# A hybrid attention layer: the output projection by Strassen's seven products, with the weights' sums made by accumulating transfers

## The chip, the cores and the metric

The kernel runs on one core of one Trainium2 chip. Its time is the device time in microseconds of one execution. TensorE multiplies, VectorE (DVE) and ScalarE (ACT) work on tiles, GpSimd (POOL) does small vector work and issues one queue of transfers, SyncE (SP) issues the other queue.

## What is computed

The reference is one decoder layer on 512 tokens of width 2048, in float32:

```python
h = rmsnorm(x, norm_pre_g)
qa, ka, va, za, qb, ckv, zb, iq, ik, iw = split(h @ w_in)
o_a = diff_attention(qa, ka, va, ...) * silu(za)      # 8 heads of 128
o_b = dsa_attention(qb, rmsnorm(ckv), iq, ik, iw, ...) * silu(zb)  # 8 heads of 128
y = concat(o_a, o_b) @ w_out                          # 512 x 2048 by 2048 x 2048
return x + rmsnorm(y, norm_post_g)
```

The change concerns the product with `w_out`.

## The kernel before, in words

Every large product is made of float32r matmuls with both operands split into a high and a low part: high times high, high times low, low times high, so three matmuls stand for one. The split is a ScalarE copy to float32r (the high part) and a VectorE subtraction (the low part).

The weights pass through one stream. A list `units` (lines 54 to 81) names every weight block in order of use, 128 x up to 1024 elements each. `load_to` (line 89) issues their loads on SyncE's queue into the tiles `wf` (two buffers), `split_to` (line 103) splits them into `wh` and `wl` (lines 123 and 124, three buffers each), and `use` (line 128) hands out the next unit and moves loads and splits ahead. Inside `lead()` these instructions get a priority up to 600 places earlier, so the scheduler, which orders each engine's instructions at build time by priority and by its own model of time, puts them before their use. The engines then run their orders without changing them.

After the projections come eight heads of group A (lines 547 to 563) and eight of group B (lines 576 to 583). The scheduler lays the projections of the next heads over the softmax of the last ones. In group A each head ends with a norm: a sum of squares through TensorE (lines 508 to 512, the square in the tile `sq`), a power of -0.5 on POOL (`rstd`, line 195), and four transposes on TensorE that spread the result over the partitions (`spread`, line 201), before `go[h]` is scaled (line 516). `go[0..7]` holds group A's output and `go[8..15]` group B's, each 128 features x 512 tokens. The bias strips of the heads come through a DRAM table that POOL's queue writes (`strip`, lines 330 to 336); `sc` holds the selection masks of group B, `pt0a` to `pt3b` the transposed probabilities.

Before the last head, fifteen of the sixteen tiles `go` are split for the projection (`split_o`, line 569, into `hh` and `hl`); the last one after it. The projection (lines 589 to 660) goes over four blocks of 512 columns. For each of eight units of weights (two slices of 128 features) it runs four row tiles of 128 tokens, three matmuls each (lines 600 to 602). `done` (line 604) squares the result on ScalarE with a row sum and multiplies it by the gain. In the last block (lines 619 to 660) the row tiles follow one another, each 48 matmuls (the last one in two halves of 256 columns), and each is finished at once: norm, residual from `xn`, and stores to `out`. The last block's weights are kept in tiles that the heads have left (`last`, line 101).

Of the kernel before, what the change touches and what calls it, by code (L numbers as in the profile page):

```python
# [26 lines left out]
def hybrid_layer(tc, xT, xn, wck, wT, wva, wuv, wo, vecs, gpost, lams, relb, oneh, out):  # L27
    nc = tc.nc
    from contextlib import ExitStack
    with ExitStack() as st:  # L30
# [48 lines left out]
        for n in range(4):  # L79
            for kp in range(8):  # L80
                unit(wo[n, kp], (2, 512))
        stage, ready, flags = {}, {}, {"begin": None}
# [5 lines left out]

        def load_to(n):
            while pos["load"] < min(n, len(units)):  # L90
# [3 lines left out]
                nm, bf = ("wf", 2) if flags["begin"] is not None else ("qk", 4)  # L94
# [6 lines left out]
        last = [("qk", 4)] * 4 + [("v", 3)] * 3 + [("ck0", 1), ("ck1", 1)] + [("wh", 3), ("wl", 3)] * 3 + [("pt0a", 1)]  # L101

        def split_to(n):
            while pos["split"] < min(n, len(units)):
                i = pos["split"]
                load_to(i + 1)
                c = units[i][1][0] * units[i][1][1]
                t = stage.pop(i)
                names = [("wh", 3), ("wl", 3)]
                if i >= len(units) - 8:  # L110
                    names = [last.pop(0), last.pop(0)]
                w = []
                for nm, bf in names:
                    if nm == "pt0a":
                        w.append([S.tile([128, 512], F32R, name=x, bufs=1) for x in ("pt0a", "pt0b")])
                    else:
                        a = S.tile([128, 1024], F32R, name=nm, bufs=bf)
                        w.append([a[:, :512], a[:, 512:]] if units[i][1][1] == 512 else [a[:, :c]])
                m = c // len(w[0])
                with tc.high_priority(lead()):  # L120
                    for q in range(len(w[0])):
                        src = t[:, q * m:(q + 1) * m]
                        nc.scalar.copy(w[0][q], src)  # L123
                        nc.vector.tensor_tensor(w[1][q], src, w[0][q].bitcast(F32), op=OP.subtract)  # L124
                ready[i] = w
                pos["split"] += 1

        def use(ahead=3):
            i = pos["use"]
            pos["use"] += 1  # L130
            if ahead:
                load_to(i + ahead + 1)
                split_to(i + ahead)
            nk, n = units[i][1]
            w = ready.pop(i)
            per = nk // len(w[0])
            return [[w[a][k // per][:, (k % per) * n:(k % per + 1) * n] for k in range(nk)] for a in range(2)]
# [55 lines left out]
        def rstd(dst, ssq, n):  # L193
            nc.vector.tensor_scalar(dst, ssq, 1.0 / n, EPS, op0=OP.mult, op1=OP.add)
            nc.gpsimd.tensor_tensor(dst, dst, mhalf[:, :dst.shape[1]], op=OP.pow)
# [167 lines left out]
        def select():  # L363
            for i in range(1, 4):
                nc.gpsimd.affine_select(sc[i][:, i * 128:], sc[i][:, i * 128:], [[-1, 128]], OP.is_ge, -BIG,
                                        base=0, channel_multiplier=1)
# [136 lines left out]
        def head_a(h, q, k, kl):  # L503
# [3 lines left out]
            sq = tmp("sq", 1)  # L507
# [38 lines left out]

        for h in range(8):
            next(sel, None)
            if h % 2 == 0:
# [17 lines left out]
        oh_, ol_ = [], []  # L567

        def split_o(m):
            a = S.tile([128, 512], F32R, name=f"hh{m}")  # L570
            b = S.tile([128, 512], F32R, name=f"hl{m}")
            split((a, b), go[m])
            oh_.append(a)
            ol_.append(b)
# [12 lines left out]
        ssy = S.tile([128, 4, 4], F32, name="ssy")  # L587
        ys = {}
        for n in range(4):
            gB = S.tile([128, 512], F32, name="strip", bufs=2)  # L590
# [137 lines left out]
```

## Time and profile before

| | before |
|---|---|
| median of three executions | 1054.93 us (1054.83 to 1055.67) |
| the profiled execution, its own time | 1055.42 us |
| its span, first to last instruction | 1053.6 us |
| matmuls | 5425, busy 99% of the span |
| granted TensorE clock, mean | 0.998 |
| VectorE, ScalarE, POOL busy | 54%, 40%, 3% of the span |
| moved by transfers | 116 MB, 110 GB/s on average |

All rows come from the profiled execution. PE is TensorE's matmuls, PEld its weight loads, which run beside them. Matmul records overlap one another, because the next one starts before the last has drained. A row of the timeline gives the start from the span's beginning, the duration, the engine, the line, the operation, its output and inputs, and in brackets the idle time before it with what ended it.

### The profile page before, as it was taken

What the parts mean: (1) busy time and instruction counts of PE and PEld (TensorE: products, weight loads), DVE (VectorE), ACT (ScalarE), POOL (GpSimd) and SP (SyncE); (2) the same over time, 40 slices, a digit from 0 to 9 for tenths busy, and PEclk for the clock granted to TensorE, in tenths of its full rate; (3) what the DMA queues carried; (4) which work ended last, traced back from release to release, by engine and by line L of the source; (5) the groups of instructions that cost most, each with busy time, mean ns of one, the idle gap of its engine ahead of it and who ended that gap; (6) DMA issues with size and microseconds to landing.
All of it is one profiled execution on the core that took longest, in us unless ns stands there. A gap on an engine that the chain in (4) does not pass through costs nothing.

```text
span 1053.6 us, 13903 instructions
## 1 busy us (share of the span) xinstructions
PE 1042.1 (99%) x5425; PEld 897.7 (85%) x5425; DVE 568.0 (54%) x1143; ACT 420.9 (40%) x788; POOL 30.3 (3%) x48
## 2 busy tenths in 40 slices
PE   9999999999999999999999999999999999999997
PEld 6798888988889899899899888888888888888886
DVE  6255554569943474565565466554645484323353
ACT  6543433432223464464464465333323353322320
POOL 0002000000000000000000000000000000000001
PEclk9999999999999999999999999999999999999999
DMA  9535633223222322322222232231223232233445
GB/s 347 203 100 177 227 100 100 86 96 100 91 94 95 100 75 86 98 73 91 82 89 86 75 110 81 84 98 60 92 79 94 77 109 91 91 100 110 137 132 191
DMA packets 37073, 116.09 MB, mean 110 GB/s; under 512 B 4448, under 2 KB 4704, under 8 KB 37008
## 3 DMA queue, kind: packets, MB, share of 16 engines
q1 hardware_dynamic: 35376, 108.88, 32.0%
q0 software_dynamic: 1632, 6.33, 1.9%
q8 instruction: 42, 0.69, 0.3%
q14 instruction: 23, 0.19, 0.1%
HBM read 110.96 MB, written 9.48 MB: 114 GB/s over the span
## 4 chain that ended last, share of the span: by engine, by line
PE 97%; DMA 2%; ACT 0%; DVE 0%; issue 0%; SPq 0%; DVEq 0%; POOL 0%; POOLq 0%; ACTq 0%
PE pj L162 19%; PE pj L161 19%; PE pj L160 19%; PE pj L445 3%; PE pj L444 3%; PE pj L443 3%; PE lg L528 3%; PE av L426 3%; PE pj L600 2%; PE pj L602 2%; PE pj L601 2%; PE tr L415 2%; PE lg L252 2%; PE lg L254 2%; DMA wf<-in_wT_dram 1%; PE lg L602 1%
## 5 line engine op out<-in xcount | busy, mean ns | idle before, releaser
L162 PE MATMUL pj<-hh,wl 128*128 128x512 f32 (+2 forms) x912 | 351.9, 386 | 0.0
L161 PE MATMUL pj<-hl,wh 128*128 128x512 f32 (+2 forms) x912 | 350.8, 385 | 0.0
L160 PE MATMUL pj<-hh,wh 128*128 128x512 f32 (+2 forms) x912 | 350.3, 384 | 0.0
L123 ACT CAST wh<-wf 128x1024 fp32r<-128x1024 f32 (+1 forms) x179 | 162.9, 923 | 389.8 <-PE pj L161 182.5
L124 DVE TENSOR_TENSOR wl<-wf,wh 128x1024 fp32r<-128x1024 f32 (+1 forms) x179 | 189.2, 1068 | 196.6 <-ACT wh L123 196.3
L162 PEld LDWEIGHTS pj<-hh,wl 128*128 128x128 f32 (+1 forms) x912 | 170.7, 187 | 30.8 <-issue 0.9
L161 PEld LDWEIGHTS pj<-hl,wh 128*128 128x128 f32 (+1 forms) x912 | 170.6, 187 | 29.9
L160 PEld LDWEIGHTS pj<-hh,wh 128*128 128x128 f32 (+1 forms) x912 | 170.8, 187 | 29.2
L445 PE MATMUL pj<-wh,hl 128*128 128x256 f32 x256 | 73.0, 285 | 0.0
L443 PE MATMUL pj<-wh,hh 128*128 128x256 f32 x256 | 72.9, 285 | 0.0
L444 PE MATMUL pj<-wl,hh 128*128 128x256 f32 x256 | 72.7, 284 | 0.0
L258 DVE SCALAR_TENSOR_TENSOR tq<-pj,rB 128x512 f32<-128x512 f32 (+1 forms) x40 | 26.6, 664 | 66.1 <-PE pj L162 64.4
L444 PEld LDWEIGHTS pj<-wl,hh 128*128 128x128 f32 x256 | 48.9, 191 | 0.6
L443 PEld LDWEIGHTS pj<-wh,hh 128*128 128x128 f32 x256 | 48.9, 191 | 0.4
L445 PEld LDWEIGHTS pj<-wh,hl 128*128 128x128 f32 x256 | 48.8, 191 | 0.1
L601 PE MATMUL pj<-wl,hh 128*128 128x512 f32 x96 | 37.5, 391 | 0.0
L528 PE MATMUL lg<-ck,qk 128*128 128x256 f32 (+3 forms) x192 | 37.4, 322 | 0.0
L600 PE MATMUL pj<-wh,hh 128*128 128x512 f32 x96 | 37.3, 391 | 0.0
L602 PE MATMUL pj<-wh,hl 128*128 128x512 f32 x96 | 37.2, 390 | 0.0
L528 PEld LDWEIGHTS lg<-ck,qk 128*128 128x128 f32 x192 | 32.0, 189 | 3.5
L538 ACT ACTIVATE a<-a,mx 128x128 f32<-128x128 f32 (+3 forms) x32 | 17.9, 561 | 38.5 <-DVE mx L537 38.5
L397 DVE SCALAR_TENSOR_TENSOR sc<-e,iw,sc 128x256 f32<-128x256 f32 (+2 forms) x45 | 27.7, 615 | 7.4 <-ACT e L393 4.8
(343 smaller groups left out, 1414.9 us busy)
## 6 DMA issues: line engine op xcount, KB each, us to landing
wf<-in_wT_dram SPq DMA_DIRECT2D x111, 512.0 KB, 3.5
wf<-in_wo_dram SPq DMA_DIRECT2D x32, 512.0 KB, 3.5
wf<-in_wva_dram SPq DMA_DIRECT2D x16, 512.0 KB, 3.5
table<-bd POOLq DMA_DIRECT2D x16, 320.0 KB, 11.1
go<-in_xT_dram SPq DMA_DIRECT2D x16, 256.0 KB, 6.1
v<-in_xn_dram SPq DMA_DIRECT2D x8, 512.0 KB, 5.1
strip<-table SPq DMA_DIRECT2D x16, 256.0 KB, 3.4
out_dram<-go SPq DMA_DIRECT2D x16, 256.0 KB, 3.6
```

The costliest lines, as they stand in the source:

```text
L123: nc.scalar.copy(w[0][q], src)
L124: nc.vector.tensor_tensor(w[1][q], src, w[0][q].bitcast(F32), op=OP.subtract)
L160: nc.tensor.matmul(ps, a, x, start=(k == 0), stop=False)
L161: nc.tensor.matmul(ps, a, y, start=False, stop=False)
L162: nc.tensor.matmul(ps, b, x, start=False, stop=(k == KT - 1))
L443: nc.tensor.matmul(o, hh[kk][:, ts], wh[k], start=(kk == 0 and i % 2 == 0), stop=False)
L444: nc.tensor.matmul(o, hh[kk][:, ts], wl[k], start=False, stop=False)
L445: nc.tensor.matmul(o, hl[kk][:, ts], wh[k], start=False, stop=(kk == 15 and i % 2 == 1))
L528: nc.tensor.matmul(bank[:, :w], q[u][:, x, i * 128:(i + 1) * 128], ck[u][:, y, :w], start=(n == 0), stop=(n == 5))
L600: nc.tensor.matmul(banks[i], oh_[kk][:, ts], wh[k], start=(kk == 0), stop=False)
L601: nc.tensor.matmul(banks[i], oh_[kk][:, ts], wl[k], start=False, stop=False)
L602: nc.tensor.matmul(banks[i], ol_[kk][:, ts], wh[k], start=False, stop=(kk == 15))
```

## The change

The 512 x 2048 activations are cut into quarters (256 tokens x 1024 features: A11 and A12 are the first 256 tokens of groups A and B, A21 and A22 the last 256), and for each half of the output columns (a pass `p`) the weights are cut into four blocks of 1024 features x 512 columns. Each pass then takes seven products of quarters in place of eight: `a11`, `a12`, `a22`, `d1` = A22 - A21, `e2` = d1 + A11, `s3` = e2 - A22 and `s4` = e2 - A12, each with one weight block or one sum T1 to T4 of blocks. The seven results are added up to the four output blocks.

- The sums T1 to T4 lie in DRAM tiles `tw`. `combine` makes them by transfers on POOL's queue: four copies and four accumulations for each pass and each of four units, 64 transfers of 512 KB. One step is issued in each head (`sums`), behind POOL's last instruction so far: four copies and two accumulations in the heads 0, 2, 4 and so on, two accumulations in the others.
- The stream has 56 units for the projection instead of 32. `wf` gets three buffers instead of two, and `ck1` as a fourth after the heads. Only two units are loaded before the last head has been written down, since the others may read `tw`.
- The activations' sums are made by VectorE and POOL: `d1` in `go[h]` after each head of group B (on POOL, in the last head on VectorE); `e2`, `s3` and `s4` after the last head, eight slices through two temporaries each, then split into tiles that the heads have left.
- A product is 2 row tiles x 8 slices x 3 matmuls. Its result is copied (ScalarE) or subtracted (VectorE, some on POOL) into tiles. The last product of the second pass runs row tile by row tile, the second one in halves.
- `sq` takes a buffer of the ring `tq`.

```diff
-        for n in range(4):
-            for kp in range(8):
-                unit(wo[n, kp], (2, 512))
+        plain = len(units)
+        B11, B12, B21, B22, T1, T2, T3, T4 = range(8)
+        tw = {(p, f, u): DR.tile([128, 1024], F32, name=f"tw{p}{f}{u}")
+              for p in range(2) for f in (T1, T2, T3, T4) for u in range(4)}
+        ORDER = ((("a11", B11), ("d1", T1), ("e2", T2), ("s3", T3), ("s4", B22), ("a22", T4), ("a12", B21)),
+                 (("a11", B11), ("e2", T2), ("s3", T3), ("a22", T4), ("d1", T1), ("s4", B22), ("a12", B21)))
+        for p in range(2):
+            for _, f in ORDER[p]:
+                for u in range(4):
+                    unit(wo[p, f, u] if f < 4 else tw[p, f, u], (2, 512))
+        ring = [("wf", 3)] * 3
...
+        def combine(p, u):
+            def add(dst, src):
+                nc.gpsimd.dma_start(tw[p, dst, u], wo[p, src, u] if src < 4 else tw[p, src, u], accum_op=OP.add,
+                                    max_dma_last_dim=1024)
+            for dst, src in ((T1, B11), (T3, B12), (T2, B11), (T4, B21)):
+                nc.gpsimd.dma_start(tw[p, dst, u], wo[p, src, u])
+            add(T1, B12)
+            add(T3, B22)
+            yield
+            add(T2, T3)
+            add(T4, T2)
+            yield
...
-            sq = tmp("sq", 1)
+            sq = tmp()
...
+        combos = (None for p in range(2) for u in range(4) for _ in combine(p, u))
+        def sums():
+            with tc.issue_after(flags["pool"].ins):
+                next(combos)
         for h in range(8):
             next(sel, None)
+            sums()
...
         for h in range(8):
             if h % 2 == 0:
                 project_vb(h // 2)
+            sums()
             q = [project_qk(1.0 / 16), project_qk(1.0 / 16)]
             if h == 7:
-                for m in range(15):
-                    split_o(m)
+                for j in range(7):
+                    split_x(j, slice(0, 512))
+                split_x(7, lo)
             head_b(h, q)
-        split_o(15)
+            eng = nc.gpsimd if h < 7 else nc.vector
+            flags["pool"] = eng.tensor_tensor(go[h][:, up], go[8 + h][:, up], go[h][:, up], op=OP.subtract)
+        flags["limit"] = len(units)
+        ring.append(("ck1", 1))
+        split_x(7, up)
...
+        for j in range(8):
+            t = S.tile([128, 512], F32, name=("pt0b", "sc3")[j % 2])
+            s3 = S.tile([128, 256], F32, name=("pt2a", "pt2b")[j % 2])
+            nc.vector.tensor_tensor(t[:, up], go[j][:, up], go[j][:, lo], op=OP.add)
+            nc.gpsimd.tensor_tensor(s3, t[:, up], go[8 + j][:, up], op=OP.subtract)
+            nc.gpsimd.tensor_tensor(t[:, lo], t[:, up], go[8 + j][:, lo], op=OP.subtract)
+            z = S.tile([128, 2, 512], F32R, name=zhome[j][0], bufs=zhome[j][1])
+            split((z[:, 0, :], z[:, 1, :]), t)
+            split((ws[j][:, 0, :], ws[j][:, 1, :]), s3)
...
+        def product(form):
+            ps = [bank(), bank()]
+            for u in range(4):
+                w = use()
+                for i in range(2):
+                    part(ps[i], form, i, u, w)
+            return ps
...
+            P1 = product("a11")
+            for i in range(2):
+                nc.scalar.copy(ra[i], P1[i])
+            if p == 0:
+                P5 = product("d1")
+                for i in range(2):
+                    nc.scalar.copy(rb_[i], P5[i])
+                P6 = product("e2")
+                for i in range(2):
+                    sub(rc_[i], P6[i], ra[i])
+                P7 = product("s3")
+                for i in range(2):
+                    sub(rd[i], rc_[i], P7[i])
+                    sub(rc_[i], rc_[i], rb_[i], nc.gpsimd)
+                    sub(rb_[i], rd[i], rb_[i], nc.gpsimd)
+                    done(rb_[i], 2 + i, n2, gBs[1])
...
+                cuts = (0, 512) if i == 0 else (0, 256, 512)
                 for a, b in zip(cuts, cuts[1:]):
...
+                    ps = bank()[:, cs]
+                    for u in range(4):
+                        part(ps, "a12", i, u, w[u], cs)
+                    nc.vector.tensor_tensor(ra[i][:, cs], ps, ra[i][:, cs], op=OP.add)
+                    square(ra[i][:, cs], i, n1)
+                    more(ry if b == 512 else base, i, n1, base)
+                    nc.vector.tensor_tensor(ra[i][:, cs], ra[i][:, cs], gBs[0][:, cs], op=OP.mult)
+                final(i, ry, xs[i])
```

In the first pass the products run in the order `a11`, `d1`, `e2`, `s3`, `s4`, `a22`, `a12`; in the second `a11`, `e2`, `s3`, `a22`, `d1`, `s4`, `a12`. `part` is the three matmuls for each of a unit's two slices, `done` and `final` are as before. `zhome` puts the split sums into the tiles `qk` (four), `v` (three) and `ck0`; the splits of `s3` go into `kz`, `tq`, `e`, `rB` and `pt0a`.

## Rows read from the trace of the kernel before

**Rows 1.** Page, busy shares, granted clock by slice, and the chain by engine:

```profile
PE 1042.1 (99%) x5425; PEld 897.7 (85%) x5425; DVE 568.0 (54%) x1143; ACT 420.9 (40%) x788; POOL 30.3 (3%) x48
PEclk9999999999999999999999999999999999999999
PE 97%; DMA 2%; ACT 0%; DVE 0%; issue 0%; SPq 0%; DVEq 0%; POOL 0%; POOLq 0%; ACTq 0%
```

**Rows 2.** Window 900 to 1000 us: PE, PEld, DVE, ACT, POOL busy, clock, DMA:

```profile
900.00:1000.00 100.00, 100.00 (x443) 82.81 (x442) 31.73 (x50) 28.72 (x58) 1.09 (x2) 1.00 0.36 112
```

**Rows 3.** Page, DMA issues: count, size, median us to landing:

```profile
wf<-in_wo_dram SPq DMA_DIRECT2D x32, 512.0 KB, 3.5
table<-bd POOLq DMA_DIRECT2D x16, 320.0 KB, 11.1
```

**Rows 4.** Groups by line and shape (busy us, mean ns | idle before):

```profile
L124 DVE TENSOR_TENSOR wl<-wf,wh 128x1024 fp32r<-128x1024 f32 x127 | 155.4, 1224 | 137.7 <-ACT wh L123 137.5
L123 ACT CAST wh<-wf 128x1024 fp32r<-128x1024 f32 x127 | 133.0, 1047 | 316.0 <-PE pj L161 178.8 <-issue 108.7 <-PE pj L445 16.1
L234 DVE TENSOR_TENSOR pt2b<-tr,pt2a 128x256 fp32r<-128x256 f32 x16 | 6.7, 421 | 0.6 <-ACT pt2a L233 0.6
L608 DVE TENSOR_TENSOR go<-pj,strip 128x512 f32<-128x512 f32 x6 | 4.1, 688 | 1.5 <-ACT a L606 1.4
```

**Rows 5.** Timeline of POOL, the tables' issues (start us, us, ...):

```profile
92.11 4.16 POOL L332 DMA_DIRECT2D table<-bd  x8 [1.69 <-DMA bd<-v]
97.18 0.52 POOL L332 DMA_DIRECT2D table<-bd  x1 [0.91 <-DMA table<-bd]
```

**Rows 6.** Transfers and TensorE's waits, 92 to 130 us; landings of tile table:

```profile
q0 software_dynamic: 1280, 5.24, 48.8%
wf<-in_wT_dram SPq DMA_DIRECT2D x6, 512.0 KB, 5.4
...
PE lg L252 <- DVE v L240: 1.2, 1, 1.2
...
DMA to landing us min/median/max: 2.5/8.6/14.5
```

**Rows 7.** Timeline of POOL, the powers in the heads:

```profile
398.19 1.47 POOL L195 TENSOR_TENSOR ro<-ro,mhalf 128x4 f32<-128x4 f32 x1 [158.47 <-DVE ro L194]
418.64 1.01 POOL L195 TENSOR_TENSOR ro<-ro,mhalf 128x4 f32<-128x4 f32 x1 [18.98 <-DVE ro L194]
478.81 1.44 POOL L195 TENSOR_TENSOR ro<-ro,mhalf 128x4 f32<-128x4 f32 x1 [59.16 <-DVE ro L194]
```

**Rows 8.** Timeline of TensorE, the spreading transposes after a power:

```profile
424.01 0.60 PE L201 MATMUL av<-ident,ro 128*128 128x128 f32 x4
```

**Rows 9.** Window 861.7 to 897.9 us: all engines, then line 600 alone:

```profile
861.70:897.90 36.20, 36.20 (x179) 30.45 (x179) 18.84 (x43) 10.98 (x26) 0.55 (x1) 1.00 0.28 95
...
861.70:897.90 36.20, 15.50 (x41) 7.64 (x41) 1.00 0.28 95
```

**Rows 10.** Timelines of TensorE, then VectorE, around the last head's end:

```profile
890.30 0.49 PE L415 MATMUL tr<-ident,a 128*128 128x128 f32 x3
890.55 0.48 PE L426 MATMUL av<-pt0b,v 128*128 128x512 f32 x1
897.39 0.27 PE L426 MATMUL av<-pt3a,v 128*128 128x128 f32 x1
...
867.03 1.16 DVE L533 TENSOR_TENSOR a<-strip,sc 128x384 f32<-128x384 f32 x2 [0.67 <-PE tr L415]
892.70 0.28 DVE L234 TENSOR_TENSOR pt3b<-tr,pt3a 128x128 fp32r<-128x128 f32 x1
```

**Rows 11.** Timelines of VectorE (twice) and POOL, final row tiles:

```profile
1025.02 1.42 DVE L659 SCALAR_TENSOR_TENSOR go<-go,ry,e 128x512 f32<-128x512 f32 x2
...
1047.90 2.41 DVE L659 SCALAR_TENSOR_TENSOR go<-go,ry,tq 128x512 f32<-128x512 f32 x2
...
1048.03 1.73 POOL L657 TENSOR_TENSOR go<-sq,e 128x512 f32<-128x512 f32 x1 [0.83 <-ACT sq L656]
```

More of the change, by code (lines that the diff above doesn't have):

```diff
@@ L87, in lead @@
             return 0 if b is None else max(0, min(LEAD, tc.cur_priority - b))
+        ring = [("wf", 3)] * 3
         def load_to(n):
-            while pos["load"] < min(n, len(units)):
+            while pos["load"] < min(n, len(units), flags["limit"]):
                 i = pos["load"]
@@ L126, in split_to @@
+                per = nk // len(w[0])
+                ready[i] = [[x[k // per][:, k % per * n1:(k % per + 1) * n1] for k in range(nk)] for x in w]
                 pos["split"] += 1
@@ L131, in use @@
             if ahead:
-                load_to(i + ahead + 1)
+                load_to(i + ahead + (3 if i >= plain else 2))
                 split_to(i + ahead)
[L134 to L137, printed above, removed]
+            return ready.pop(i)
         warm = S.tile([128, 1], F32, name="warm")
@@ L565, in hybrid_layer, with split_x @@
             pass
[L567 to L574, printed above, removed]
+        lo, up = slice(0, 256), slice(256, 512)
+        pairs, F = [], {}
+        def split_x(j, cs):
+            if j == len(pairs):
+                pairs.append([S.tile([128, 512], F32R, name=f"{nm}{j}") for nm in ("hh", "hl")])
+            a, b = pairs[j]
+            split((a[:, cs], b[:, cs]), go[j][:, cs])
         for h in range(8):
@@ new lines, in sub, with square, done, others @@
+        def sub(dst, a, b, eng=None):
+            (eng or nc.vector).tensor_tensor(dst, a, b, op=OP.subtract)
+        def square(y, i, n):
+            junk = S.tile([128, 512], F32, name="pt0b")
+            w = y.shape[1]
+            nc.scalar.activation(junk[:, :w], y, AF.Square, accum_out=ssy[:, i, n:n + 1])
+        def done(y, i, n, gB):
+            square(y, i, n)
+            nc.vector.tensor_tensor(y, y, gB, op=OP.mult)
+            ys[i, n] = y
+        def others(i, n):
+            base = S.tile([128, 1], F32, name="base", bufs=2)
+            c, d = [x for x in range(4) if x != n][1:]
+            nc.vector.tensor_tensor(base, ssy[:, i, 0:1], ssy[:, i, c:c + 1], op=OP.add)
+            nc.vector.tensor_tensor(base, base, ssy[:, i, d:d + 1], op=OP.add)
+            nc.vector.tensor_scalar(base, base, 1.0 / D, EPS, op0=OP.mult, op1=OP.add)
+            return base
@@ new lines, in more, with final @@
+        def more(dst, i, n, base):
+            nc.vector.scalar_tensor_tensor(dst, ssy[:, i, n:n + 1], 1.0 / D, base, op0=OP.mult, op1=OP.add)
+        def final(i, ry, xs):
+            nc.gpsimd.tensor_tensor(ry, ry, mhalf[:, 0:1], op=OP.pow)
+            for q in range(4):
+                if i == 1 and q == 1:
+                    t = S.tile([128, 512], F32, name="sc3")
+                    nc.scalar.activation(t, ys[i, q], AF.Copy, scale=ry)
+                    nc.gpsimd.tensor_tensor(ys[i, q], t, xs[q], op=OP.add)
+                else:
+                    nc.vector.scalar_tensor_tensor(ys[i, q], ys[i, q], ry, xs[q], op0=OP.mult, op1=OP.add)
+                nc.sync.dma_start(out[i * 128:(i + 1) * 128, q * 512:(q + 1) * 512], ys[i, q])
```

203 lines of the change are left out of this document (112 added, 91 removed).

## The prediction

> **What bounds the kernel now.** I first read the busy shares, then the chain that ended last, then the stretch that is changed. TensorE is busy 99% of the span at the full granted clock, and 97% of the chain is matmuls [rows 1]; so time is won only by fewer matmuls, and lost by whatever makes TensorE wait. The records of single matmuls overlap, so their mean is no price. The cadence is: between 900 and 1000 us, where TensorE runs nothing but the projection's 512-column matmuls, 443 start in 100 us [rows 2], 0.2257 us each. VectorE and ScalarE are busy there 32 and 29 us of the 100 [rows 2].
>
> **What is removed.** Before, the projection is 4 column blocks x 4 row tiles x 16 slices x 3 = 768 matmuls. After, it is 2 passes x 7 products x 2 row tiles x 8 slices x 3 = 672. So 96 x 0.2257 = **21.7 us** less. The last row tile stays cut into halves in both, which costs the same.
>
> **Weights.** 56 units instead of 32 pass through load, ScalarE copy and VectorE subtraction, one per 12 matmuls = 2.71 us instead of 5.42. A load lands 3.5 us after issue [rows 3], the copy takes 1.05 and the subtraction 1.22 [rows 4]. With four buffers a slot comes round every 10.8 us and needs 5.8, so I cost it at nothing; SyncE's 24 further issues are queued in the same way. What hides it is 5.1 us of slack; if the cover goes, the bound is below under the fourth rival. A product then asks VectorE for 4 x 1.22 plus two evictions with two 0.69 us operations each (2.8) [rows 4], 7.7 of its 10.8 us: covered, and the ScalarE squares and copies are fewer.
>
> **The sums of the weights, during the heads.** 64 transfers of 512 KB go from POOL, 32 copies and 32 accumulations. No such transfer is in the trace. The nearest is the 320 KB DRAM-to-DRAM copy of the tables, issued in 0.52 us: eight are issued from 92.11, and the ninth issue waits for one to land until 97.18, so the first lands in 5.1 us at most [rows 5]; the median is 11.1 with eight queued [rows 3]. For 512 KB that is 8.1 us, and 17.8 when queued. An accumulation also reads its target: 16.2 as my middle value, ends 3.5 (a plain load) and 35.6.
> Two things stand behind it. First POOL's own queue: an accumulation must wait for the transfer whose result it adds, and POOL stands in that wait. Behind it in the heads of group A is the power of -0.5 (line 195), and behind that TensorE's spreading transposes. The eight powers come in four pairs, the first at 398.19 and 418.64, the next from 478.81 [rows 7]. A step of the sums is put behind each. The long gap of about 59 us gets four copies and two accumulations, the short one, 19.0 us from the end of one power to the next, two accumulations of which the second waits for the first. That costs 0.5 + 16.2 + 0.5 us: it fits. Even a late power is not at once late for TensorE: the power at 418.64 ends at 419.65, and its transposes start at 424.01 [rows 8], 4.4 us later. So an accumulation may take 19.0 - 1.0 + 4.4 = 22.4 us before TensorE waits, and then each of the four short gaps costs the excess. I take nothing.
> Second the bandwidth: the worst burst before, 5.24 MB of table copies among six weight loads from 92 to 125 us, landed those loads in 5.4 us at the median, and TensorE waited 1.2 us [rows 6]. Three load buffers instead of two give 3 x 5.42 - 1.05 - 1.22 - 3.5 = 10.5 us of slack to a load in the heads. Nothing, with 1 us as the end for each of eight bursts. The square's buffer, now out of the ring of `tq`, overlaps no two live tiles in the order seen: nothing.
>
> **The transition, where I expect a stall.** Between 861.7 and 897.9 us, TensorE fills the latency of the last heads with 41 + 40 + 40 = 121 projection matmuls, 27.3 us (one of the three lines stands in the rows, the others count 40); the other 8.9 are heads' work [rows 9]. After the change only the first product (48) and seven of eight slices of the second (42) are free of the last head: 90 x 0.2257 = 20.3 us. TensorE runs out at 861.7 + 20.3 + 8.9 = 890.9.
> The last head's final transposes are at 890.30, their evictions end at 892.98, its last matmul starts at 897.39, with filler in between [rows 10]. Without filler I take 892 as its end.
> Then come the sums of activations for the third product. For each of 8 slices VectorE does an addition (0.42), a 512-wide (0.69) and a 256-wide subtraction (0.42) [rows 4], 1.53 us; POOL does two 256-wide subtractions. POOL's 512-wide addition took 1.73 us, but beside it two VectorE operations took 2.41 instead of 1.42 [rows 11]: the two engines hold each other up. POOL started at 1048.03 while the first operation ran to about 1048.65, so it may have needed only 1.1 us by itself, 0.55 to 0.87 for 256; I take 0.6.
> The temporaries of slices 0 and 1 are `pt0b` and `sc3`, whose last readers (890.55, and 867.03 + 1.16) are gone earlier [rows 10]; so two slices can be ready by 892. For six: 0.7 for the gate, 6 x 1.53 = 9.2, and four units' subtractions, 4.9: 892 + 14.8 = 906.8 if POOL works beside VectorE, 914.0 if its 12 x 0.6 = 7.2 us come on top. After that six matmuls remain, 1.4 us: the third product ends between 908.2 and 915.4. TensorE alone would end it at 861.7 + 8.9 + 144 x 0.2257 = 903.1. The **stall** is 5.1 to 12.3 us; I take the middle, **8.7**. Ends: 0 if the scheduler gets the sums out early, 17.7 if nothing is ready by 892 and all is in series (892.7 + 12.2 + 9.6 + 4.9 + 1.4 = 920.8). The later products have their sums by then.
> The Trainium skill, "SBUF — State Buffer", section "Who interferes with whom", says that a VectorE instruction with two SBUF inputs and a GpSimd instruction that reads SBUF contend for one shared read interface, and that the second blocks wholly until the first is done. By that rule the stall would be the series value of 12.3 us; the pair in [rows 11] shows a delay of 1.0 us for a POOL operation of 1.73, between the two.
>
> **The tail.** After the last matmul an addition of 0.42 us stands before the square. The last two row tiles now follow each other after 24 matmuls (5.5 us) instead of 48, so the first one's four operations of 0.71 and its stores crowd the second's: 0.5 by estimate from these rows [rows 4, 11]. **+1.0**, ends 0 and 2.5.
>
> **Sum.** -21.7 + 8.7 + 1.0 = -12.0. The profiled execution took 1055.42 us (span 1053.6): 1043.4. It stands 0.5 above the median 1054.93; against that I predict **1042.9**.
>
> **Rivals.**
> (1) *The stall is hidden.* For it: the filler of the first two products is 21.7 us, and VectorE was busy only 18.84 of the 36.2 us there [rows 9]; against it: buffers that the last head frees last. -21.7 + 1.0 gives 1034.2. Chance 0.13.
> (2) *Accumulations hold POOL too long: slower.* Place: POOL's queue between paired powers. It decides from 22.4 us per accumulation, and eats the whole gain from 22.4 + 12.0/4 = 25.4. At 30 us: 4 x 7.6 = 30.4, so 1073. For it: of the tables and their loads the slowest took 14.5 us to land [rows 6], for 512 KB and doubled 46; against: the first landed in 5.1. Chance 0.10.
> (3) *VectorE and POOL exclude each other fully*, as they half do in [rows 11], and no slice is early: stall 17.7, 1051.9. Chance 0.10. The Trainium skill's rule above would give this if it held throughout.
> (4) *Supply is the new bound of the projection.* If a unit takes 3.1 us instead of 2.71, 56 x 0.39 = 21.8 goes back, 1056 with a stall hidden. For it: VectorE carries splits, evictions and final rows together; in the second pass's last products I count 22.5 us against 21.7. Against: 112 GB/s take 0.36 of the transfer engines now [rows 2]; the 194 that are wanted would take 0.62. Chance 0.05.
>
> **How the numbers follow.** My forecast, stall 3 to 15 us (1037 to 1049), has 0.62. The range 1033.5 to 1052 takes in rivals 1 and most of 3, about 0.82. A measurement tells 0.2% (2.1 us) from no change; below 1052.8 counts as faster. Faster: 0.62 + 0.13 + most of 3 = 0.83. Same: the rest of 3 and a little of 2 and 4, 0.05. Slower: 0.12.
>
> **What the profile after would show.** Right: 672 projection matmuls at 0.226 us; TensorE idle some 9 us between 890 and 915 waiting for VectorE, POOL or ScalarE results of the sums, none in the heads; the powers of -0.5 still about 20 and 59 us apart; accumulations landing under 22 us; loads under 6. Wrong: idle TensorE before the spreading transposes (rival 2); no idle near 900 (rival 1); waits for weight copies throughout the projection (rival 4).

## The result and the profile after

The changed kernel takes **1066.3 us** (median of 4 runs, 1064.7 to 1068.4), the kernel before beside it 1055.3: a ratio of 1.0105, with a 95% interval of 1.0083 to 1.0127. It is slower by 11 us where 12 us less were predicted, and lies above the range. The profiled run, the quickest of the four, took 1064.73 us with a span of 1062.9. Of the variant d_order further down one run of four took 1457.8 us at a mean granted clock of 0.654, and its figures leave this run out.

The busy shares and the granted clock by slice, as in [rows 1] of the kernel before:

```profile
span 1062.9 us, 13966 instructions
...
PE 1035.9 (97%) x5305; PEld 885.9 (83%) x5305; DVE 624.8 (59%) x1194; ACT 452.9 (43%) x807; POOL 111.7 (11%) x139
...
PE   9999999999999999999999999999999999799995
...
PEclk9999999999999999999999999999999999899998
```

TensorE has 97% of a longer span instead of 99%, and in slice 35, about 904 to 930 us, it has 0.7 of the time and a clock below its upper level. The last matmul of a head's projection and the last matmul of all (start us, us, engine, line) part the span into three, first in the kernel before, then after:

```profile
860.98 0.39 PE L162 MATMUL pj<-hh,wl 128*128 128x512 f32 x1
...
1045.53 0.28 PE L644 MATMUL pj<-wl,hl 128*128 128x256 f32 x1
```

```profile
874.07 0.39 PE L185 MATMUL pj<-hh,wl 128*128 128x512 f32 x1
...
1051.15 0.28 PE L668 MATMUL lg<-hh,go 128*128 128x256 f32 x1
```

| | before | after | difference |
|---|---|---|---|
| heads: last projection matmul starts | 860.98 | 874.07 | +13.1 |
| from there to the end of the last matmul | 184.8 | 177.4 | -7.4 |
| from there to the end of the span | 7.8 | 11.5 | +3.7 |
| span | 1053.6 | 1062.9 | +9.3 |

The 96 matmuls less should have shortened the middle by 21.7 us, so 14.3 are lost there. Of the three losses the first, in the heads, was forecast as nothing.

**The heads.** TensorE waited for nothing between 330 us and the transition before; now it does (engine, tile and line waited for, sum, times, longest):

```profile
PE tr L535 <- ACT tq L531: 3.4, 5, 0.7
PE pj L668 <- DVE hl L257: 2.0, 1, 2.0
PE lg L666 <- ACT v L256: 1.8, 1, 1.8
PE pj L666 <- ACT hh L256: 1.5, 1, 1.5
...
PE tr L438 <- DVE a L522: 1.2, 1, 1.2
```

The first and the last line lie in the heads, the three between them behind the heads. The first is the square that ends an A head. The 10 us windows (their length, TensorE busy, its instructions, granted clock, DMA share, GB/s) show what such gaps cost:

```profile
610.00:620.00 10.00, 10.00 (x48) 1.00 0.90 183
620.00:630.00 10.00, 7.35 (x46) 1.00 0.30 101
630.00:640.00 10.00, 10.00 (x48) 0.83 0.53 105
...
660.00:670.00 10.00, 10.00 (x48) 1.00 0.43 131
670.00:680.00 10.00, 8.85 (x39) 0.83 0.46 159
...
900.00:910.00 10.00, 7.78 (x38) 1.00 0.48 162
910.00:920.00 10.00, 6.81 (x20) 0.83 0.23 64
920.00:930.00 10.00, 8.25 (x24) 0.66 0.25 93
930.00:940.00 10.00, 9.93 (x43) 1.00 0.53 157
```

Over all windows of 10 us from 330 to 880 TensorE is idle for 6.1 us, and the share that the clock falls short of its upper level adds up to 5.1 us: 11.2 in all. From the first head's first evacuation (340.06 before, 338.48 after, below) to the last projection the loss is 14.7; 3.5 us are in neither sum. A part of them is how idle time is counted, from the end of a record: at the first square TensorE's matmuls start at 385.82 and 386.78 us, 0.96 us apart where 0.07 is usual for this shape, and 0.69 of it count as idle. For 11 waits this makes about 2 us, an estimate; the rest stays open.

**Where the pairs went.** VectorE's evacuations of a projection into the ring `tq` and ScalarE's squares, first in the kernel before (L258, L508), then after (L281, L531), there also the last matmul of the second key's projection (L185):

```profile
340.06 0.69 DVE L258 SCALAR_TENSOR_TENSOR tq<-pj,rB 128x512 f32<-128x512 f32 x1 [3.31 <-PE pj L162]
...
350.94 0.69 DVE L258 SCALAR_TENSOR_TENSOR tq<-pj,rB 128x512 f32<-128x512 f32 x1 [3.31 <-PE pj L162]
...
362.34 0.69 DVE L258 SCALAR_TENSOR_TENSOR tq<-pj,rB 128x512 f32<-128x512 f32 x1 [1.37 <-PE pj L162]
...
374.88 0.69 DVE L258 SCALAR_TENSOR_TENSOR tq<-pj,rB 128x512 f32<-128x512 f32 x1 [0.73 <-PE pj L162]
```

```profile
394.11 0.60 ACT L508 ACTIVATE sq<-av 128x512 f32<-128x512 f32 x1 [1.23 <-PE av L426]
```

```profile
338.48 0.69 DVE L281 SCALAR_TENSOR_TENSOR tq<-pj,rB 128x512 f32<-128x512 f32 x1 [3.32 <-PE pj L185]
...
349.35 0.69 DVE L281 SCALAR_TENSOR_TENSOR tq<-pj,rB 128x512 f32<-128x512 f32 x1 [3.31 <-PE pj L185]
...
385.52 0.68 DVE L281 SCALAR_TENSOR_TENSOR tq<-pj,rB 128x512 f32<-128x512 f32 x1
...
388.34 0.68 DVE L281 SCALAR_TENSOR_TENSOR tq<-pj,rB 128x512 f32<-128x512 f32 x1
```

```profile
372.86 0.39 PE L185 MATMUL pj<-hh,wl 128*128 128x512 f32 x1
```

```profile
386.13 0.60 ACT L531 ACTIVATE tq<-av 128x512 f32<-128x512 f32 x1 [0.85 <-PE av L449]
```

Before, the query and the key of the second head (362.34, 374.88) were evacuated 32 and 19 us before the first head's square (394.11). After, they come at 385.52 and 388.34, around the square (386.13), though TensorE has had both products ready since 373 us. So the second head's logits start only when the first head is nearly done, and the softmax of one no longer runs beside the last matmuls of the other. The powers, which started 20 and 60 us apart in [rows 7], now start 32 to 47 us apart, and no two of them form a pair; the first three:

```profile
388.51 1.03 POOL L218 TENSOR_TENSOR ro<-ro,mhalf 128x4 f32<-128x4 f32 x1 [143.33 <-DVE ro L217]
435.51 1.04 POOL L218 TENSOR_TENSOR ro<-ro,mhalf 128x4 f32<-128x4 f32 x1 [38.59 <-DVE ro L217]
471.81 1.03 POOL L218 TENSOR_TENSOR ro<-ro,mhalf 128x4 f32<-128x4 f32 x1 [27.83 <-DVE ro L217]
```

**What was right.** The transfers of the sums land fast and hold nothing up (compare [rows 3]; count, KB, median us to landing):

```profile
tw<-in_wo_dram POOLq DMA_DIRECT2D x48, 512.0 KB, 7.3
wf<-tw SPq DMA_DIRECT2D x24, 512.0 KB, 3.7
...
tw<-tw POOLq DMA_DIRECT2D x16, 512.0 KB, 5.9
```

### The profile page after: what moved, and what is told of

It reads as the page before. It is cut to its first block, busy times and chain, and to the rows that moved or that the text cites. A ratio compares the mean times of both kernels' runs of the same rounds, so it can differ in the third digit from the quotient of the medians.

```text
span 1062.9 us, 13966 instructions
## 1 busy us (share of the span) xinstructions
PE 1035.9 (97%) x5305; PEld 885.9 (83%) x5305; DVE 624.8 (59%) x1194; ACT 452.9 (43%) x807; POOL 111.7 (11%) x139
## 4 chain that ended last, share of the span: by engine, by line
PE 95%; DVE 2%; ACT 1%; issue 1%; POOL 1%; DMA 0%; SPq 0%; DVEq 0%; POOLq 0%
PE pj L183 19%; PE pj L184 19%; PE pj L185 19%; PE pj L466 3%; PE pj L467 3%; PE pj L468 3%; PE lg L551 3%; PE av L449 3%; PE pj L667 2%; PE pj L668 2%; PE pj L666 2%; PE lg L277 2%; PE lg L275 2%; PE tr L438 2%; PE lg L666 1%; PE lg L667 1%
## 5 line engine op out<-in xcount | busy, mean ns | idle before, releaser
L185 PE MATMUL pj<-hh,wl 128*128 128x512 f32 (+2 forms) x912 | 352.0, 386 | 0.0
L148 ACT CAST wh<-wf 128x1024 fp32r<-128x1024 f32 x171 | 177.4, 1037 | 319.4 <-PE pj L184 145.3
L149 DVE TENSOR_TENSOR wl<-wf,wh 128x1024 fp32r<-128x1024 f32 x171 | 209.8, 1227 | 159.6 <-ACT wh L148 158.9
L185 PEld LDWEIGHTS pj<-hh,wl 128*128 128x128 f32 (+1 forms) x912 | 171.3, 188 | 30.6 <-issue 0.9
L281 DVE SCALAR_TENSOR_TENSOR tq<-pj,rB 128x512 f32<-128x512 f32 (+1 forms) x40 | 26.3, 661 | 39.3 <-PE pj L185 37.2
L218 POOL TENSOR_TENSOR ro<-ro,mhalf 128x4 f32<-128x4 f32 x8 | 8.3, 1032 | 371.4 <-DVE ro L217 371.4
L551 PE MATMUL lg<-ck,qk 128*128 128x384 f32 (+3 forms) x192 | 37.5, 322 | 0.0
L561 ACT ACTIVATE a<-a,mx 128x128 f32<-128x128 f32 (+3 forms) x32 | 17.9, 561 | 40.7 <-DVE mx L560 40.7
L438 PE MATMUL tr<-ident,a 128*128 128x128 f32 x160 | 30.5, 273 | 1.6 <-DVE a L522 1.2
L518 ACT ACTIVATE a<-a,mx 128x128 f32<-128x128 f32 (+3 forms) x32 | 18.0, 563 | 29.4 <-DVE mx L517 29.1
```

Source lines behind the costliest of these rows:

```text
L148: nc.scalar.copy(x, src)
L149: nc.vector.tensor_tensor(y, src, x.bitcast(F32), op=OP.subtract)
L185: nc.tensor.matmul(ps, b, x, start=False, stop=(k == KT - 1))
L438: nc.tensor.transpose(bank[:, (i - j) * 128:(i - j + 1) * 128], a[i][:, j * 128:(j + 1) * 128], ident)
L551: nc.tensor.matmul(bank[:, :w], q[u][:, x, i * 128:(i + 1) * 128], ck[u][:, y, :w], start=(n == 0), stop=(n == 5))
```

## The experiments

Theories: **A**, the ring costs the heads; **B**, the sums' transfers do; **C**, the third staging buffer and the new order of loads do. For the stretch after the heads: **D**, order of the splits; **E**, VectorE and GpSimd hold each other up; **F**, weights held back; **G**, the work of the activations' sums. For the end: **H**, late last weights. All runs in three parts, worked out from the starts and ends of matmuls as above (medians of several runs, the rest from the profiled one):

| kernel | median | last projection | then to last matmul | then to end | span |
|---|---|---|---|---|---|
| before | 1055.3 | 861.0 | 184.8 | 7.8 | 1053.6 |
| after | 1066.3 | 874.1 | 177.4 | 11.5 | 1062.9 |
| b_sq_ring | 1070.3 | 877.3 | 184.8 | 7.8 | 1069.9 |
| b_sums | 1055.7 | 861.5 | 184.8 | 7.8 | 1054.1 |
| a_no_sums | 1064.7 | 876.2 | 175.2 | 11.6 | 1062.9 |
| a_sq_own | 1051.3 | 860.3 | 176.8 | 11.1 | 1048.2 |
| c_late | 1049.1 | 860.5 | 174.5 | 11.0 | 1046.0 |
| c_dve | 1050.9 | 860.0 | 177.0 | 11.0 | 1048.0 |
| s_none | 1040.4 | 859.2 | 165.0 | 12.3 | 1036.4 |
| d_order | 1046.3 | 860.8 | 172.8 | 11.0 | 1044.5 |
| e_order4 | 1047.2 | 861.0 | 173.4 | 11.1 | 1045.4 |
| e_rhythm | 1046.5 | 860.1 | 173.2 | 11.3 | 1044.6 |
| c_fin | 1053.5 | 861.8 | 179.9 | 11.6 | 1053.3 |
| d_tail | 1053.2 | 860.8 | 182.5 | 8.8 | 1052.1 |
| e_rtail | 1048.1 | 860.2 | 175.2 | 9.0 | 1044.4 |
| c_all | 1050.6 | 861.1 | 177.3 | 11.5 | 1049.9 |
| d_best | 1047.4 | 861.1 | 175.7 | 8.8 | 1045.6 |

### The heads

**b_sq_ring**, the kernel before with

```diff
-            sq = tmp("sq", 1)
+            sq = tmp()
```

and the last stage's one other user of `sq` moved to another free tile.

> The kernel before, with one thing changed: the square that ends an A head lies in the ring of two buffers of the evacuated projections, as in the changed kernel. Theory A (the ring: the key projection of the next A head can't be evacuated before the square of the head before has been read, so the heads can no longer be worked in pairs, and TensorE gets gaps): slower by 9 to 16 us, about 1067 beside 1055, with the last head's last projection matmul near 873 us instead of 861 and waits of TensorE for the square. Theory B (the sums' transfers disturb the heads): no change, 1055. Theory C (three staging buffers and another order of loads disturb the heads): no change, 1055.

Measured 1070.3, ratio 1.0134 (1.0112 to 1.0157): 15 us slower, as theory A said. Everything is lost in the heads (+16.3 us by the profile), nothing behind them. Its waits:

```profile
PE tr L512 <- ACT tq L508: 3.4, 5, 0.7
PE tr L415 <- DVE a L499: 1.2, 1, 1.2
```

The same 3.4 us in 5 waits as in the changed kernel, by one line. Theory A is shown; B and C can't explain it.

**a_sq_own**, the changed kernel with that line undone, and for the room:

```diff
-        ring = [("wf", 3)] * 3
+        ring = [("wf", 2)] * 2
```

(loads one unit less ahead).

> The changed kernel with the square in a buffer of its own again; to make room for it the staging ring has two buffers again and loads run one unit less ahead. Theory A: the heads come back to the time of before, the last head's last projection near 861 us, and the whole is faster by about 12 us, near 1054; the transition and the end keep their losses. Theory B: stays at 1066. Theory C: also back near 1054, so that this run parts A from B alone and the run with the kernel before and the ring alone parts A from C.

Measured 1051.3, ratio 0.9964 (0.9949 to 0.9979): 15 us faster than the changed kernel and faster than the one before. The heads are back to 860.3. This run also takes one staging buffer away, so by itself it doesn't part A from C; b_sq_ring does, where the staging is as it was.

**a_no_sums**, the changed kernel without the transfers:

```diff
-                unit(wo[p, f, u] if f < 4 else tw[p, f, u], (2, 512))
+                unit(wo[p, f % 4, u], (2, 512))
...
-            with tc.issue_after(flags["pool"].ins):
-                next(combos)
+            pass
```

> The changed kernel without the 64 transfers that make the weights' sums; the units that read a sum read a plain block of the weights of the same size instead (the output projection is computed with wrong factors, the amount of work is the same). Theory A: the same, 1066, heads as slow as in the changed kernel. Theory B: the heads come back, about 1054. Theory C: the same, 1066.

1064.7, ratio 1.0076 (1.0047 to 1.0105), with the heads as slow as before this edit (876.2). The profiled runs of both have the same span, 1062.9, and the 1.6 us between the medians lie within the spread of the runs (1061.0 to 1066.6 here).

**b_sums**, the kernel before with the changed kernel's `combine` (on its own blocks) and in each head of both loops

```diff
+            sums()
```

> The kernel before with the 64 transfers of the sums added in its heads, issued on GpSimd after the latest power as in the changed kernel; the sums are made of equal blocks of the weights as they lie in this kernel, and nothing reads them. Theory A: no change, 1055. Theory B: slower by about 12 us, 1067, with the last head's last projection near 873 us. Theory C: no change, 1055.

1055.7, ratio 0.9998 (0.9986 to 1.0010): nothing, though the transfers landed more slowly here, in 10.0 and 9.6 us. B falls, from both sides.

### The stretch behind the heads

**c_late** and **c_dve** start from a_sq_own. The first queues the splits of the right halves behind the last split of a sum:

```diff
-            split((y, small), go[8 + j])
+            with tc.issue_after(sums_cast.ins):
+                split((y, small), go[8 + j])
```

> The changed kernel with the square's own buffer (its run: span 1048.2 us, 14.1 us without a matmul or at the lower clock between 870 and 930 us), and the splits of the right halves, which only the fifth to seventh product read, queued on ScalarE behind the last split of a sum. Theory D (order: TensorE runs out of work after the heads because VectorE and ScalarE work off these 8 splits, some 5.4 us of VectorE's rows, ahead of the sums that the third and fourth product need): 3 to 6 us faster, near 1044 by the profile. Theory E (contention: GpSimd's subtractions and VectorE's instructions lengthen each other): within 1 us of 1048. Theory F (supply: the weights of the first products come late, since their loads are held to two units until the last head is done): within 1 us of 1048.

1049.1, span -2.2: less than D said, and not clear of the spread of the runs, since its ratio, 0.9940 (0.9919 to 0.9961), overlaps that of a_sq_own. TensorE is idle for as long as without the edit (8.3 us between 870 and 930, against 8.5). In a_sq_own the clock falls short by another 1.7 us between 900 and 910 us, and here it doesn't; the windows do not give the 14.1 us named above.

The second puts the sums' subtractions on VectorE:

```diff
-            nc.gpsimd.tensor_tensor(s3, t[:, up], go[8 + j][:, up], op=OP.subtract)
-            nc.gpsimd.tensor_tensor(t[:, lo], t[:, up], go[8 + j][:, lo], op=OP.subtract)
+            nc.vector.tensor_tensor(s3, t[:, up], go[8 + j][:, up], op=OP.subtract)
+            nc.vector.tensor_tensor(t[:, lo], t[:, up], go[8 + j][:, lo], op=OP.subtract)
```

> The changed kernel with the square's own buffer and the 16 subtractions of the sums on VectorE instead of GpSimd. In the run without this, VectorE's instructions beside GpSimd's took 0.53 us more each, 5.3 us in all over 11 of them; on VectorE the 16 cost 16 x 0.42 = 6.7 us. Theory D: 1 to 3 us slower (VectorE has more to do, in the same order). Theory E: 2 to 4 us faster, because also the chains of sum, subtraction and split get shorter. Theory F: within 1 us.

1050.9, span -0.2: no gain, no loss, as F said, where D and E expected a change. TensorE is idle for 8.9 us against 8.5, without the fall of the clock. So ending the contention buys nothing here: with VectorE alone at the same sums the stretch is as long.

**s_none** leaves the activations' sums out; the loop over `t`, `s3`, `z` and `ws` becomes

```diff
+            F["s4", j], F["e2", j] = ([t[:, cs] for t in pairs[j]] for cs in (lo, up))
+            F["s3", j] = F["e2", j]
```

> The changed kernel with the square's own buffer, without the activations' sums: the products that read a sum read the splits of the left halves instead, so the 8 additions, 16 subtractions and 16 splits of the sums are left out (the output projection is computed with wrong factors, TensorE's work is the same). Theory G (the stall after the heads is the work of these sums on VectorE, GpSimd and ScalarE): TensorE's idle time between 870 and 930 us falls from 8.5 us to about 4 (what the last head's own chain and the splits of the right halves leave), the whole is 3 to 6 us faster, span 1042 to 1045. Theory F (the loads of the weights, held until the last head ends): idle time stays over 7 us, span 1047 to 1048.

Span 1036.4, 11.8 us less than a_sq_own (10.9 by the medians); twice what G said. TensorE's waits from 862 to 930 us are then

```profile
PE av L449 <- ACT pt0a L256: 0.8, 1, 0.8
PE pj L659 <- DVE wl L149: 0.5, 1, 0.5
PE tr L438 <- DVE pt0b L257: 0.2, 1, 0.2
```

1.5 us, and the middle stretch is 165.0, within 1.9 of the 163.1 that 21.7 us off 184.8 would give. So nearly the whole stall comes with these sums; F falls, since the loads are held as before. The run takes away two things at once, the work on the engines that also split TensorE's weights and the third product's wait for its sum; the next three runs try to part them.

**d_order** puts the product of plain right halves third on the first two columns:

```diff
-("a11", B11), ("d1", T1), ("e2", T2), ("s3", T3), ("s4", B22), ("a22", T4), ("a12", B21)
+("a11", B11), ("d1", T1), ("a12", B21), ("e2", T2), ("s3", T3), ("s4", B22), ("a22", T4)
```

with its splits made in the last head.

> The changed kernel with the square's own buffer, and on the first two columns the product that reads the plain right halves put third instead of last (its splits made during the last head, in the buffers that its last projection has freed), so that 10.8 us of matmuls (48 at 0.226 us) stand ahead of the first product that needs a sum. Theory G: 4 to 8 us faster than 1048.2, since the sums get that much more time; the idle time of TensorE between 870 and 930 us falls below 4 us. Theory F: within 1.5 us of 1048.

1046.3, ratio 0.9917 (0.9901 to 0.9932). Span -3.7, just short of G's 4 to 8 (4.9 by the medians). But TensorE is still idle for 6.5 us, where G said less than 4. What remains:

```profile
PE lg L671 <- DVE wl L149: 4.0, 3, 2.2
PE tr L671 <- DVE wl L149: 1.0, 1, 1.0
PE av L449 <- ACT pt0a L256: 0.8, 1, 0.8
```

What is left of TensorE's waits is nearly all for VectorE's halves of *weights* (`wl`), not for a sum.

**e_order4** puts the other plain product fourth:

```diff
+("a11", B11), ("d1", T1), ("a12", B21), ("a22", T4), ("e2", T2), ("s3", T3), ("s4", B22)
```

> As the run with the right halves' product third, and the other product of plain right halves put fourth on the first two columns (its result kept in two buffers until the difference that it needs exists), so that 43 us of matmuls (4 products of 48 at 0.226 us) stand ahead of the first that needs a sum. Theory G1 (what is left of the stall, 4.0 us of waits for the weights' low parts between 900 and 915 us, comes from the sums standing ahead of the weights' splits on VectorE, whoever needs them first): no change, span 1043 to 1046. Theory G2 (the sums are needed too soon): 3 to 5 us faster, span 1040 to 1042.

1047.2, the same 4.0 us of waits for `wl`: G2 falls, and more distance to the first sum buys nothing. **e_rhythm** also makes the sums one by one, in the products `d1` and `a12`:

```diff
                 w = use()
+                if sums:
+                    with tc.issue_after(flags["sub"].ins):
+                        make_sum(sums[u])
```

where `sub` is VectorE's part of the latest unit's split.

> As the run before it, and the eight sums queued on VectorE one behind each weight unit's split during the second and third product. One sum costs VectorE about 0.41 + 0.68 + 0.41 = 1.5 us and a unit's split 1.22 us, 2.7 together, and a unit feeds TensorE for 12 x 0.226 = 2.7 us. Theory G1: the 4.0 us of waits for the weights' low parts fall below 2 us, span 1040 to 1043. Theory G2 or another: no change.

1046.5, with 2.9 us in that wait instead of 4.0. G1 had the direction right, but it said below 2 us and a span of 1040 to 1043, and the span is 1044.6, 0.8 less than in the run before. The likely reason is VectorE's total load: from 900 to 920 us it is busy for 19.9 us in d_order and e_order4 and for 20.0 in e_rhythm, where s_none has 12.4. An order can't hide what fills the engine. Part of this busy time is VectorE's own instructions lengthened by GpSimd's, and no run tells how much of the wait that is, since none has the new order without GpSimd.

### The end

**c_fin** queues the first row tile's closing instructions behind the second's last sum of squares (`m`):

```diff
-                final(i, ry, xs[i])
+            with tc.issue_after(m.ins):
+                final(0, rys[0], xs[0], False)
+            final(1, rys[1], xs[1], False)
```

with the power of -0.5 taken out of `final`.

> The changed kernel with the square's own buffer, and in the last stage the four closing instructions of the first row tile queued on VectorE behind the last sum of squares of the second. Between the last matmul (1037.2) and the end (1048.2) lie 11.0 us, against 7.8 in the kernel before. If this order on VectorE holds the end (the second row tile's power waits 2.4 us for four closing instructions): 1.3 to 2.5 us faster. If the number of closing instructions after the last matmul holds it (seven on VectorE, 0.7 to 1.2 us each): less than 0.7 us.

The power of the second tile starts 1.7 us after the last matmul instead of 4.0, and the stretch to the end is 11.6 us as ever: the seven closing instructions on VectorE still stand behind the last matmul, the last of them until 1049.3, and their stores after that. So the number of closing instructions holds the end, the second of the two forecasts. The whole is 1053.5, and in the profiled run the stretch behind the heads was worse (between 860 and 930 us idle for 9.2 us and short of clock by 5.1, against 8.5 and 1.7). Up to the last stage the order of instructions is that of a_sq_own; why it ran worse here stays open.

**d_tail** changes the order on SyncE and TensorE in the last stage (`load` and `mm` are the latest load and the latest matmul):

```diff
-                xs[i] = residual(i, ...)
+                with tc.issue_after(flags["load"].ins):
+                    xs[i] = residual(i, ...)
...
-                    for u in range(4):
-                        part(ps, "a12", i, u, w[u], cs)
+                    with tc.issue_after(flags["mm"].ins):
+                        for u in range(4):
+                            part(ps, "a12", i, u, w[u], cs)
```

> The changed kernel with the square's own buffer; in the last stage the residual's 8 loads for the first two row tiles are queued on SyncE behind the last weight load, and the second row tile's matmuls of the last product on TensorE behind the first's. Theory H (the end is long because the last weights come late beside the residual's loads, TensorE mixes both row tiles while it waits, and then 7 closing instructions of both stand behind the last matmul): the stretch from the last matmul to the end falls from 11.0 us to about 8, as in the kernel before, and the whole is 2 to 3 us faster, span 1045 to 1046. If the stretch is set by something else: no change, or up to 1 us slower by the order forced on TensorE.

The end is 8.8 us, as H said, but TensorE waits 2.0 us for late halves of weights in the last product, and the middle is 5.7 us longer: 1053.2, nothing gained. About half of the 5.7 lies behind the heads, far from the edit (idle for 9.7 us against 8.5, short of clock by 3.4 against 1.7). **e_rtail** is e_rhythm with d_tail's edit, the residual behind both last loads.

> As the run before it; in the last stage the residual's 8 loads for the first two row tiles are queued on SyncE behind both last weight loads (in the earlier run two of them still stood ahead of one), and the second row tile's matmuls behind the first's. Theory H (late last weights make the end long): TensorE waits less than 1 us in the last product and the stretch from the last matmul to the end is about 9 us instead of 11, so 1.5 to 2.5 us faster than the run before it. If the loads are bound by their buffers or by the stores and not by the residual: TensorE waits 2 to 3 us and nothing is gained.

End 9.0 instead of 11.3, middle 175.2 instead of 173.2. The last weights' copies are now done by 1024 us instead of 1027.6, and still TensorE waits 2.5 us:

```profile
PE pj L672 <- DVE hl L149: 2.5, 2, 2.0
```

VectorE is late with their low halves. H is half right: the mixed order did cost 2 us at the end, but undoing it moves the wait into the product.

**c_all** (c_late, c_dve, c_fin)

> The three edits together, on the changed kernel with the square's own buffer. If each is worth what its theory says, 1048.2 - 4.5 - 2 - 1.5 = about 1040 us by the profile; if only the order of the splits counts, near 1044; if the stall after the heads is held by the loads of the weights, 1047.

gave 1050.6 (span 1049.9), above all three of its forecasts, and **d_best** (d_order with d_tail's edits)

> Both edits, the third product and the end, on the changed kernel with the square's own buffer: by theories G and H 1048.2 - 6 - 2.5 = about 1040 us of span; against the kernel before a ratio near 0.987. By F alone 1045.

gave 1047.4, ratio 0.9922 (0.9909 to 0.9934): no better than d_order alone. Its span of 1045.6 is near what F alone would give, but s_none had ruled F out. The best versions, d_order, e_order4, e_rhythm and d_best, can't be told apart by their intervals; they are 0.8% faster than the kernel before, d_order 1.9% faster than the changed one.

## Why the prediction was wrong

- **The failing step** is one sentence: "The square's buffer, now out of the ring of `tq`, overlaps no two live tiles in the order seen: nothing." It looked at the order of the kernel before and asked whether two live tiles would share a buffer there. But the program asks the ring for its two buffers in turn, for the query, the key and the square of one head, then for the next head's. So the second key gets the buffer that the first square held, and can be evacuated only when that is read, as the rows have it (386.13, then 388.34). The second query gets the first key's buffer, which was read by 353 us, and yet it came at 385.52, 0.6 us before the square; that the order made at build time hands out the buffers in the program's order would explain it, and no row shows it. The order seen, with the second head's evacuations up to 32 us ahead of the first head's square, was possible only because the square was outside: b_sq_ring moves nothing else in the heads. The term was not 0 but +13.1 us in the changed kernel, +16.3 alone. No rival had it: rival 2 had the right sign with the wrong mechanism, and b_sums rules it out.
- **The matmuls less**: right. Without the sums' work the middle shrinks by 19.8 us, against 21.7.
- **The stall**: right in place and cause, and TensorE's idle time there came near the size: 8.7 us predicted, 7.2 measured between 900 and 940 us, 8.5 with the heads mended. But the loss was 14.3 (13.7 with the heads mended), above the likely 5.1 to 12.3. The missing term is the clock: after the gaps 512-column matmuls start every 0.43 us instead of 0.23 (922.3 to 927.5 us), and the clock falls short by 1.7 us in the window from 910 and by 3.4 in the one from 920 us; with the heads mended by 1.7. Another 2.0 (3.5) us are in neither sum, in part because idle time is counted from the end of a record. Without the clock the losses are 9.2 and 12.0, so the choice of the middle between side by side and one after the other (5.1 and 12.3) is not decided. GpSimd's subtraction took 0.72 us by itself, not 0.6.
- **The tail**: +1.0 predicted with an end at 2.5, +3.7 measured. Mis-sized: both last row tiles end within 1.3 us of each other, since TensorE mixes them while the last weights arrive, so seven closing instructions on VectorE instead of three stand behind the last matmul.
- **The sums' transfers, rival 2**: nothing, as predicted; 16.2 us per accumulation was more than twice too much. The accumulations among DRAM tiles landed in 5.9 us at the median, and no transfer of the sums took more than 12.3. The wait of 1.2 us in [rows 6], read as the price of a burst, names VectorE's tile `v`, not a load.
- **Rivals 1, 3 and 4**: the stall was not hidden. It did not reach rival 3's 17.7 us; the collisions that this rival names are in the trace, but c_dve, which has none, loses as much. And supply is not the bound of the later products. From 930 to 1000 us TensorE is full in all runs on a_sq_own, and loads land in 3.7 us, as predicted.
- Together, by the profiles: -21.7 + 13.1 + 14.3 + 3.7 = +9.4 us, against 9.3 of the span. Without the one line (and with two staging buffers) the kernel takes 1051.3 us: inside the range, at its upper end, for the stall and the tail were both sized too small.
- Of the signs that the prediction named, two failed, and both point at the heads: the powers no longer come in pairs, and TensorE is idle there.

## What to carry to other kernels

A buffer ring couples everything that draws from it, in the order in which the program asks. Before a tile is moved into a ring to save room, ask not whether two live tiles collide in the order seen, but what now runs ahead of it only because its buffer was elsewhere. And work that is moved to the side engines is free only where they don't also feed TensorE: here 8 sums cost about half of what 96 matmuls gave (10.9 of 21.7 us).

## What the runs showed of the hardware

GpSimd's subtraction of 128x256 takes 0.72 us by itself. Beside VectorE it lasts until VectorE leaves a gap. In d_tail, first GpSimd, then VectorE (start us, us, ...):

```profile
905.37 3.05 POOL L638 TENSOR_TENSOR pt2a<-pt0b,go 128x256 f32<-128x256 f32 x1 [3.84 <-DVE pt0b L637]
908.37 0.72 POOL L639 TENSOR_TENSOR pt0b<-pt0b,go 128x256 f32<-128x256 f32 x1
```

```profile
905.14 1.22 DVE L149 TENSOR_TENSOR wl<-wf,wh 128x1024 fp32r<-128x1024 f32 x1
906.28 0.41 DVE L637 TENSOR_TENSOR sc<-go 128x256 f32<-128x256 f32 x1
906.61 1.22 DVE L149 TENSOR_TENSOR wl<-wf,wh 128x1024 fp32r<-128x1024 f32 x1
```

Three VectorE instructions with two operands from SBUF follow each other from 905.14 to 907.83, and the subtraction needs 3.05 us. In a_sq_own the same instruction took 1.91, since the third of them started at 907.25 instead. The other way round, a VectorE split of 0.68 us takes 1.22 beside GpSimd:

```profile
906.70 0.68 DVE L257 TENSOR_TENSOR qk<-sc,qk 128x512 fp32r<-128x512 f32 x1
...
910.10 1.22 DVE L257 TENSOR_TENSOR go<-go,hl 128x512 fp32r<-128x512 f32 x1
```

```profile
909.92 0.85 POOL L638 TENSOR_TENSOR pt2a<-pt0b,go 128x256 f32<-128x256 f32 x1 [0.96 <-DVE kz L257]
```

The Trainium skill, "SBUF — State Buffer", section "Who interferes with whom", says that a VectorE instruction with two inputs in SBUF contends with a GpSimd instruction that reads SBUF, and that the one that comes second is blocked until the first is done; the trace agrees, and here GpSimd waited through three of them. c_dve, which has all of the sums in series on VectorE, is no slower. A collision of this kind decides on 1.1 us in one chain, and may be why a_sq_own spreads more from run to run (1049.6 to 1054.8 in 10 runs) than c_dve (1049.8 to 1051.4 in 4); that was not tried by itself.

The other surprise is the clock. In [rows 1] it was at its upper level (2.4 GHz) nearly throughout. Now some windows in which TensorE was idle for 0.7 to 3.2 us, or the ones behind them, show 0.61 to 0.94, so parts of them ran at the lower level (1.2 GHz). In b_sq_ring:

```profile
610.00:620.00 10.00, 10.00 (x47) 1.00 0.26 66
620.00:630.00 10.00, 8.03 (x41) 0.88 0.35 119
630.00:640.00 10.00, 9.31 (x37) 0.61 0.11 27
640.00:650.00 10.00, 10.00 (x52) 1.00 0.25 80
```

Here 2.7 us of idle time in two windows come with 5.1 us of missing clock. Not every gap did that: in d_order 3.8 us idle between 900 and 910 us left the clock at 1.00.
